# Layer 1 attention: four scheduled lanes become one list of 72 slots, with the engines held to the order of the text

## The chip, the cores and the metric

The kernel runs on one core of one Trainium2 chip. A core has five engines with instruction queues of their own: TensorE (PE, with its weight loads shown apart as PEld), VectorE (DVE), ScalarE (ACT), GpSimd (POOL) and SyncE (SP, which issues most transfers). The metric is the device time in microseconds: the median of the runs of one kernel. A profile is one execution, taken by the hardware profiler.

## The reference, cut to what matters

The program is a trunk of two layers on 1024 frames of width 1024. The change lies in layer 1, chunked softmax attention of 16 heads of 64, each chunk of 64 frames against itself and the 8 chunks before it:

```
qkv = (h @ w_qkv).reshape(bsz, seq, 3, C_HEADS, C_HEAD_DIM)
q = rmsnorm(qkv[:, :, 0], q_g) * (C_HEAD_DIM ** -0.5)
k = rmsnorm(qkv[:, :, 1], k_g)
v = qkv[:, :, 2]
...
s = jnp.einsum('bqhd,bkhd->bhqk', q_c, k_b).astype(jnp.float32) + bias
s = jnp.where(valid, s, -jnp.inf)
prob = jax.nn.softmax(s, -1).astype(v.dtype)
return jnp.einsum('bhqk,bkhd->bqhd', prob, v_b)
...
mix = chunk_band_attention(h, ...) @ attn_w_out[o]
x = x + mix
hf = rmsnorm(x, norm_ffn_g[i])
x = x + jnp.square(jax.nn.relu(hf @ mlp_w1[i])) @ mlp_w2[i]
x = x + rmsnorm(p[i] @ ple_w_proj[i], ple_norm_g[i]) * jax.nn.sigmoid(x @ ple_w_gate[i])
```

Numbers are split into a high and a low part of a narrower type, so a dense product is three matmuls (high by high, high by low, low by high), scores and values two.

## The kernel before, in words

Layer 1's input part is `layer1_in`. It works in 16 steps: `s = 2*pr + hf` is a pair of heads `pr` (0 to 7) and a half `hf` of the frames, four tiles of 128 frames. A step has four blocks, one for each head `h` of the pair and each half `blk` of the step, so there are 64 blocks, numbered `4*s + 2*h + blk`. A block takes two tiles of 128 queries (`m0` and `m0 + 1`), each against up to five tiles of 128 keys.

The work of a step, with the names that the trace shows:

- `attn_in`: the in-projection, four groups of 24 matmuls of 384 columns (`dps<-wq,act`). Each group is evicted by ACT (`qk`, line 1982, and `vs`, line 1986) and DVE (`vs`, line 1987). POOL squares q and k (`sq`, line 1994), DVE sums them (line 1995), makes one over the root with small instructions (lines 281 to 286) and multiplies (line 1998).
- `attn_norm`: eight PE transposes (`dps<-ident,qk`), first k, then q. For each, ACT makes the high part `F` (lines 2020 and 2022) and DVE the low part (line 2023: `F` for k, `Ql` for q).
- `attn_block`: for each of the two query tiles, the score matmuls into `sc`, then on DVE one custom instruction (line 2079) that adds the bias `toep` and takes the row minimum of the negated sum into `mx` (with a small read of the accumulator behind it), then the exponential on ACT (line 2081). Then PE transposes the probabilities in groups of up to 512 columns (`pt<-ident,pb`), ACT copies the high part and DVE the low part (`ptile`, lines 339 and 340), and PE multiplies them by the values into `po`. After the second block of a head `otmp` (ACT, line 2122) and `y` (DVE, line 2123) put the halves together; after the last block of a step four transposes of one over the row sums (`dps<-ident,rl`) and a multiplication (line 2132) finish `y`, which goes to memory.

The scores have one tile in the accumulation memory, two banks (`sc`); `po` has one bank, `pt` three, and two banks (`dps`) serve the in-projection, the q and k transposes, and the row-sum transposes.

What sets the order: `run` takes pieces from four generators (two lanes of blocks, one of norms, one of in-projections) by a clock of estimated latencies (the table `LAT`); what it writes down is then placed on each engine by the framework's scheduler, which goes by its own simulated times. Only the MLP, in `tail`, holds the engines to the order of the text, through the helper class `Pinned` and the flag `self.pinned`.

When the 64 groups of the in-projection are written, `attn_ins` goes on with the projection of the per-layer embedding (`ple_proj`, matmuls `dps<-act,wq` of 512 columns) and the out-projection (`out_early`), which needs the finished `y`; the MLP and the gate follow in `tail`. Ahead of it all `row_stats` makes the row norms of x from eight one-column matmuls (`dps<-ones,acc`), which read sums that POOL adds up at the end of layer 0 (line 1753).

## Time and profile before

| what | value |
|---|---|
| median of 3 runs | 3059.35 us (3057.58 to 3066.11) |
| the profiled execution's own time | 3059.3 us |
| its span, first to last instruction | 3057.6 us |
| PE busy over the span | 2948.1 us (96%) |
| first in-projection matmul of layer 1 | 1674.86 us |
| last values matmul starts its row of 11 | 2246.26 us |
| mean granted TensorE clock | 0.977 |

Times of the trace count from the first instruction. A matmul's row gives its own duration, but matmuls overlap: a row of n equal ones has one start every (row time less one duration) / (n - 1). "Idle before" is time in which an engine did nothing, with the instruction whose end let it go on; a wait shorter than the last matmul's own duration does not show as idle.

### The profile page before, as it was taken

Reading aid. Unit: us, or ns where it says so; the run is one execution under the profiler, and the core shown is the slowest. Engines: PE = TensorE matmul, PEld = TensorE weight load, DVE = VectorE, ACT = ScalarE, POOL = GpSimd, SP = SyncE. Lnnn points to the kernel's source line nnn. Section 1 sums busy time; section 2 is a strip of 40 time slices with the busy share of each in tenths; the row PEclk is TensorE's granted clock in tenths of the full one; section 3 lists DMA queues with packets and bytes.
Section 4 is the critical chain, followed back from the end, with each engine's and each line's share of the span. In section 5 each row is a group of like instructions: output and inputs, shape, how many; then the busy total and the mean of one; then the engine's idle time right before and its main releaser. Section 6 shows DMA issues by size and latency. Waiting matters only on the chain. (4 is left out here: it accounts for less than half of the span.)

```text
span 3057.6 us, 44955 instructions
## 1 busy us (share of the span) xinstructions
PE 2948.1 (96%) x16792; PEld 2473.0 (81%) x16792; DVE 2153.9 (70%) x3440; ACT 1409.1 (46%) x2546; POOL 1266.6 (41%) x1412
## 2 busy tenths in 40 slices
PE   8999999999989999999999999999999999999999
PEld 6888778887877888788888889988887888788887
DVE  5766766567758888877676566666758888877672
ACT  4444443444435544543333466655645444543331
POOL 5545533445504666644445100000204666645442
PEclk9999989999999999999999999999999999999999
DMA  4222212222444434655323111110284443654322
GB/s 129 95 86 67 68 48 74 76 66 75 163 162 165 159 150 150 245 199 172 124 90 128 65 45 41 54 44 20 81 298 167 159 151 149 240 202 174 124 94 100
DMA packets 166763, 374.29 MB, mean 122 GB/s; under 512 B 41360, under 2 KB 45584, under 8 KB 165136
## 3 DMA queue, kind: packets, MB, share of 16 engines
q1 hardware_dynamic: 134288, 312.68, 29.7%
q10 hardware_dynamic: 32256, 58.73, 5.1%
q8 instruction: 132, 2.16, 0.3%
q14 instruction: 87, 0.71, 0.1%
HBM read 259.15 MB, written 112.20 MB: 121 GB/s over the span
## 5 line engine op out<-in xcount | busy, mean ns | idle before, releaser
L173 PE MATMUL dps<-r,act 128*128 128x512 f32 x4440 | 1045.2, 394 | 10.7 <-DVE act L113 8.6
L173 PEld LDWEIGHTS dps<-r,act 128*128 128x128 f32 x4440 | 835.5, 189 | 203.5 <-DVE act L113 17.4
L173 PE MATMUL dps<-xg,whi 128*128 128x512 f32 x1248 | 420.4, 415 | 16.4 <-ACT xg L342 8.1
L113 ACT CAST act<-late 128x512 fp32r<-128x512 f32 (+1 forms) x282 | 205.5, 731 | 447.2 <-DVE late L113 258.2
L113 DVE TENSOR_TENSOR act<-late,act 128x512 fp32r<-128x512 f32 (+1 forms) x282 | 332.7, 1181 | 72.5 <-ACT act L113 69.2
L173 PE MATMUL dps<-wq,act 128*128 128x384 f32 x1536 | 301.9, 344 | 7.7 <-DVE y L2132 3.4
L173 PEld LDWEIGHTS dps<-xg,whi 128*128 128x128 f32 x1248 | 236.9, 195 | 66.8 <-ACT xg L342 8.1
L173 PEld LDWEIGHTS dps<-wq,act 128*128 128x128 f32 x1536 | 265.1, 190 | 12.7 <-DVE vs L1987 4.6
L173 PE MATMUL dps<-xg,wlo 128*128 128x512 f32 x624 | 256.4, 411 | 0.0
L113 POOL TENSOR_TENSOR late<-late 128x512 f32<-128x512 f32 (+1 forms) x104 | 186.5, 1802 | 82.4 <-ACT late L113 59.8
L113 POOL TENSOR_TENSOR late<-late,rs 128x512 f32<-128x512 f32 x88 | 137.1, 1570 | 100.9 <-DVE late L113 92.9
L1994 POOL TENSOR_TENSOR sq<-qk 128x512 f32<-128x512 f32 x32 | 34.2, 1069 | 297.1 <-ACT qk L1982 287.8
L113 DVE TENSOR_TENSOR late<-late 128x512 f32<-128x512 f32 x120 | 142.2, 1185 | 1.0
L113 DVE TENSOR_TENSOR r<-act,r 128x1024 fp32r<-128x1024 f32 (+1 forms) x80 | 138.1, 1728 | 6.7 <-ACT r L113 6.7
L173 PE MATMUL dps<-xw,act 128*128 128x512 f32 x576 | 139.2, 394 | 3.4 <-ACT act L113 3.4
L173 PEld LDWEIGHTS dps<-xg,wlo 128*128 128x128 f32 x624 | 121.3, 194 | 25.2 <-issue 0.2
L2079 DVE CUSTOM_DVE_ANT_0 pb<-sc,toep 128x640 f32<-128x640 f32 (+4 forms) x128 | 83.7, 654 | 73.4 <-PE sc L173 72.8
L173 PEld LDWEIGHTS dps<-xw,act 128*128 128x128 f32 x576 | 108.8, 189 | 28.1 <-ACT act L113 3.8
L298 ACT CAST whi<-wraw 128x1024 fp32r<-128x1024 f32 x76 | 79.5, 1048 | 86.8 <-PE dps L173 49.4
L299 DVE TENSOR_TENSOR wlo<-wraw,whi 128x1024 fp32r<-128x1024 f32 x76 | 95.1, 1252 | 33.9 <-ACT whi L298 32.8
L113 DVE TENSOR_TENSOR late<-late,dps 128x512 f32<-128x512 f32 x154 | 104.7, 682 | 19.3 <-ACT late L113 16.6
L2081 ACT ACTIVATE pb<-pb,mx 128x640 f32<-128x640 f32 (+4 forms) x128 | 89.5, 700 | 61.7 <-DVE mx L2079 55.2
(504 smaller groups left out, 5748.3 us busy)
## 6 DMA issues: line engine op xcount, KB each, us to landing
late<-in_w SPq DMA_DIRECT2D x100, 512.0 KB
hc<-late ACTq DMA_DIRECT2D x154, 256.0 KB
act<-hc SPq DMA_DIRECT2D x76, 512.0 KB
wraw<-in_w_in SPq DMA_DIRECT2D x56, 512.0 KB
hraw<-hc SPq DMA_DIRECT2D x36, 512.0 KB
hc<-sums ACTq DMA_DIRECT2D x70, 256.0 KB
act<-in_w SPq DMA_DIRECT2D x28, 512.0 KB
wraw<-in_w_out SPq DMA_DIRECT2D x21, 512.0 KB
```

The costliest lines, as they stand in the source:

```text
L113: return lambda *args, **kw: self.tc.keep_in_program_order(f(*args, **kw))
L173: r = self.nc.tensor.matmul(out, lhsT, rhs, start=start, stop=stop)
L298: nc.scalar.copy(hi, raw)
L299: nc.vector.tensor_tensor(lo, raw, hi.bitcast(F32), op=ALU.subtract)
L1994: G.tensor_tensor(sq, q4[:, 8 * e:8 * e + 8], q4[:, 8 * e:8 * e + 8], op=ALU.mult)
L2079: V.tensor_tensor_reduce(S, ps[:, o:o + n * P], toep[:, (5 - n) * P:], op0=ALU.add, op1=ALU.min, scale=-1.0, scalar=-NEG, accum_out=mx)
L2081: A.activation(S, S, AF.Exp, bias=mx, scale=-1.0, accum_out=st["l"][:, m % 4, h:h + 1])
```

## The change

The four generators go. A new function, `attention`, writes the stage as one list of 72 full slots, k from -8 to 63, and a short last one. Slot k holds the values of block k-1, the transposes of block k, the scores of block k+1, and one group of the in-projection (number k+8), whose eight pieces of three matmuls are put between the others by `fill`. When the 64 groups are used up, `fill` takes pieces of the embedding projection and then of the out-projection. Evictions, weight splits, bias loads, q and k norms and the finishing of `y` have fixed slots. Every compute instruction of PE, DVE, ACT and POOL in `attention` that goes through `self.mm`, `self.tr` or the pinned handles keeps the order of the text; the late weight and embedding work is not pinned on DVE, ACT and POOL. Three things move between engines or tiles: the small norm instructions and the scaling of q and k go from DVE to POOL (`norms`), in two halves, k first; the transposes of q, k and the row sums go from the `dps` banks to the three `pt` banks; and the eviction of v's high part is ahead of that of q and k.

```diff
     def tr(self, out, in_, ident):
         self.now += 0.107
-        return self.nc.tensor.transpose(out, in_, ident)
+        r = self.nc.tensor.transpose(out, in_, ident)
+        return self.tc.keep_in_program_order(r) if self.pinned else r
...
-            jobs = iter([(s, h, b) for s in range(16) for h in range(2) for b in range(2)])
-            self.run([self.attn_lane(steps, jobs, l1) for _ in range(2)] + [self.attn_norms(steps, l1), self.attn_ins(steps, l1)])
-
-    def attn_ins(self, steps, l1):
...
+            self.attention(l1)
...
+    def attention(self, l1):
...
+        def w_split(pr, j):
+            if j == 0:
+                W[pr] = self.weights3(pr % 2)
+            hi, lo = (w[:, j, :] for w in W[pr])
+            raw = raws.pop((pr, j))
+            A.copy(hi, raw)
+            V.tensor_tensor(lo, raw, hi.bitcast(F32), op=ALU.subtract)
...
+        def dense(d):
+            hf, e = d // 4 % 2, d % 4
+            wh, wl = W[d // 8]
+            ps = dps[d] = self.bank([P, 3, P])
+            ts = slice((4 * hf + e) * P, (4 * hf + e) * P + P)
             for k in range(NK):
...
+        def evict(d):
+            s, e = d // 4, d % 4
...
             A.activation(hi, v3, AF.Copy, scale=rc)
+            A.activation(st["qk"][:, e, :], ps[:, 0:2, :].rearrange("p a c -> p (a c)"), AF.Copy, scale=rc)
             V.scalar_tensor_tensor(vf[:, 1:3, :], v3, rc, hi.bitcast(F32), op0=ALU.mult, op1=ALU.subtract)
...
+        def squares(s, e):
+            q4 = ST[s]["qk"].rearrange("p i c -> p (i c)").rearrange("p (n d) -> p n d", d=64)
+            sq = ST[s]["sq"] = wp.tile([P, 8, 64], F32, tag="sq", name="sq", bufs=1)
             G.tensor_tensor(sq, q4[:, 8 * e:8 * e + 8], q4[:, 8 * e:8 * e + 8], op=ALU.mult)
...
+        def sums(s, e):
+            V.tensor_reduce(ST[s]["ss"][:, 8 * e:8 * e + 8], ST[s]["sq"], op=ALU.add, axis=AX.X)
+
+        def norms(s):
+            st = ST[s]
+            ss = st["ss"]
+            nn = sm.tile([P, 16], F32, tag="nn1", name="nn1")
+            w = sm.tile([P, 16], F32, tag="rswq", name="rsw")
+            G.tensor_scalar(ss, ss, 1.0 / 64, 1e-6, op0=ALU.mult, op1=ALU.add)
+            G.tensor_scalar(nn.bitcast(I32), ss.bitcast(I32), -0.5, 1597463007.0, op0=ALU.mult, op1=ALU.add)
+            for _ in range(3):
+                G.tensor_tensor(w, nn, nn, op=ALU.mult)
+                G.tensor_tensor(w, w, ss, op=ALU.mult)
+                G.tensor_scalar(w, w, -0.5, 1.5, op0=ALU.mult, op1=ALU.add)
+                G.tensor_tensor(nn, nn, w, op=ALU.mult)
+            q5 = st["qk"].rearrange("p i (j h d) -> p i j h d", j=2, h=2)
+            n4 = nn.rearrange("p (i j h) -> p i j h", i=4, j=2)
+            for j in (1, 0):
+                n = n4[:, :, j, :].rearrange("p i (h o) -> p i h o", o=1).broadcast_to((P, 4, 2, 64))
+                G.tensor_tensor(q5[:, :, j], q5[:, :, j], n, op=ALU.mult)
+
+        def bank():
+            return psm.tile([P, HB], F32, tag="pt", name="pt", bufs=3)
+
+        def heads(s, j):
+            st, qk = ST[s], ST[s]["qk"]
+            g = self.vec("kg") if j else self.dv["qg8"]
+            pt = bank()
...
+            for h in range(2):
+                r, o = halves[h], halves[1 - h]
+                A.activation(F[r, h], pt[r], AF.Copy, scale=g[r])
+                V.scalar_tensor_tensor(F[o, h] if j else lo[h][r], pt[r], g[r], F[r, h].bitcast(F32),
+                                       op0=ALU.mult, op1=ALU.subtract)
+            if not j:
+                for h in range(2):
+                    r, o = halves[h], halves[1 - h]
+                    A.activation(F[o, h], pt[r], AF.Copy, scale=g[r])
...
+        def scores(k, w):
...
+            pb = wp.tile([P, 5 * P], F32, tag="pb", name="pb", bufs=4)
+            V.tensor_tensor_reduce(pb[:, 0:n * P], ps[:, off * P:(off + n) * P], toeps[s // 2, h][:, (5 - n) * P:],
+                                   op0=ALU.add, op1=ALU.min, scale=-1.0, scalar=-NEG, accum_out=mx)
+            jb["probs"][w] = (pb, f0, mx, n, m)
+
+        def exps(k, w):
...
+            A.activation(pb[:, 0:n * P], pb[:, 0:n * P], AF.Exp, bias=mx, scale=-1.0,
+                         accum_out=ST[jb["s"]]["l"][:, m % 4, h:h + 1])
+
+        def turn(k, b):
...
+            A.copy(t[:, 0, u], pt[:, u])
+            jb["pts"][b] = (t, pt, u)
+
+        def low(k, b):
+            jb = JOB[k]
+            if b < len(jb["used"]):
+                t, pt, u = jb["pts"][b]
+                V.tensor_tensor(t[:, 1, u], pt[:, u], t[:, 0, u].bitcast(F32), op=ALU.subtract)
...
+        def values(k):
...
+        def outs(k):
...
+            A.copy(tmp[r], po[o])
+            V.tensor_tensor(st["y"][r], po[r], tmp[r], op=ALU.add)
+
+        def weigh(s):
...
+            V.reciprocal(st["l"], st["l"])
+            G.tensor_copy(rl.rearrange("p m (h i) -> p (m h) i", h=2), st["l"].rearrange("p m (h o) -> p (m h) o", o=1)
+                          .broadcast_to((P, 8, 64)))
...
+        def finish(s):
+            st = ST[s]
+            pn = bank()
+            for m in range(4):
+                self.tr(pn[:, m * P:(m + 1) * P], st["rl"][:, m, :], self.ident)
+            V.tensor_tensor(st["y"], st["y"], pn, op=ALU.mult)
...
+        def filler():
+            for d in range(64):
+                yield from dense(d)
+            yield from ple()
+            yield from out_first()
+        fl = [filler(), None]
+
+        def fill(n=1):
+            while n:
+                if fl[1] is not None and fl[1] not in self.done:
+                    return False
+                r = next(fl[0], "end")
+                if r == "end":
+                    return False
+                fl[1] = r if isinstance(r, tuple) else None
+                n -= fl[1] is None
+            return True
+
+        has = lambda k: 0 <= k < 64
...
+        for k in range(-8, 65):
+            pr, c = (k + 16) // 8, (k + 16) % 8
+            fill()
+            if has(k + 7):
+                evict(k + 7)
+            if pr < 8 and c in (1, 3, 5):
+                w_load(pr, c // 2)
+            if pr < 8 and c in (3, 5, 7):
+                w_split(pr, c // 2 - 1)
+            for h, q in ((0, k + 7), (1, k + 3)):
+                if q % 8 == 0 and has(q):
+                    toep_load(q // 8, h)
+            for h, q in ((0, k + 5), (1, k + 1)):
+                if q % 8 == 0 and has(q):
+                    toep_mask(q // 8, h)
...
+            if k % 4 == 3 and k > 0:
+                weigh(k // 4)
+            fill()
+            if has(k - 1):
+                values(k - 1)
+            fill()
+            if has(k - 1) and k % 2 == 0:
+                outs(k - 1)
+                if k % 4 == 0:
+                    finish(k // 4 - 1)
+            if k % 4 == 2 and has(k + 2):
+                heads((k + 2) // 4, 0)
+            if has(k + 5) and k % 4 == 3:
+                squares((k + 5) // 4, 0)
+            if has(k + 4) and k % 4 == 0:
+                squares((k + 4) // 4, 1)
+            if has(k + 1):
+                scores(k + 1, 0)
+            fill()
+            if has(k):
+                turn(k, 0)
+            if has(k + 1):
+                exps(k + 1, 0)
+            fill()
+            if has(k):
+                low(k, 0)
+            if has(k + 1):
+                scores(k + 1, 1)
+            if has(k + 5) and k % 4 == 3:
+                sums((k + 5) // 4, 0)
+            if has(k + 4) and k % 4 == 0:
+                sums((k + 4) // 4, 1)
+                norms((k + 4) // 4)
+            fill()
+            if has(k):
+                turn(k, 1)
+            fill()
+            if has(k):
+                turn(k, 2)
+            if has(k + 1):
+                exps(k + 1, 1)
+            if has(k):
+                low(k, 1)
+                low(k, 2)
+            if k % 4 == 1 and has(k + 3):
+                heads((k + 3) // 4, 1)
+            fill()
+            if k == -8:
+                ps = bank()
+                for i in range(NT):
+                    self.mm(ps[:, i:i + 1], self.accs[i // 4][:, (i % 4) * P:(i % 4 + 1) * P], self.ones[:, 0:1],
+                            start=True, stop=True)
+                self.row_norms(ps, self.rscol)
+        while ("ylast", 0) not in self.done:
+            fill()
+        self.split_scaled(self.ylast, ST[15]["y"], None, slice(0, HB))
+        self.done["at", 15] = 0
+        while fill():
+            pass```

The order that this gives, at the places that the prediction speaks of. In it `sc` are scores, `pt<-ident,pb` transposes of probabilities, `po` values, `dps<-wq` the in-projection, and ISA a custom instruction (with its small read behind it).

DVE, around the low parts of q (`Ql`) of one step, before:

```order
L2023 SCALAR_TENSOR_TENSOR F_17406<-dps,vecs,F_17406 64x512
L340 TENSOR_TENSOR ptile<-pt,ptile 128x512
L340 TENSOR_TENSOR ptile<-pt,ptile 128x384
L2023 SCALAR_TENSOR_TENSOR Ql<-dps,d_qg_85,F_17419 64x512
L2123 TENSOR_TENSOR y<-po,otmp 64x512
L2079 ISA pb,mx<-sc,toep 128x640
L2079 ISA mx 128x1
L2132 TENSOR_TENSOR y<-y,dps 128x512
L2023 SCALAR_TENSOR_TENSOR Ql<-dps,d_qg_85,F_17419 64x512
L2079 ISA pb,mx<-sc,toep 128x640
```

and now, in slot k with k % 4 == 2 and the slot behind it:

```order
L113 SCALAR_TENSOR_TENSOR F_18815<-pt,vecs,F_18815 64x512 x2
L113 SCALAR_TENSOR_TENSOR vs<-dps,rscol,vs 128x128
L113 TENSOR_TENSOR y<-po,otmp 64x512
L113 SCALAR_TENSOR_TENSOR Ql<-pt,d_qg_85,F_18853 64x512 x2
L113 ISA pb,mx<-sc,toep 128x384
L113 ISA mx 128x1
L113 TENSOR_TENSOR ptile<-pt,ptile 128x384
L113 ISA pb,mx<-sc,toep 128x512
L113 ISA mx 128x1
L113 SCALAR_TENSOR_TENSOR vs<-dps,rscol,vs 128x128
L113 TENSOR_TENSOR wq_18906<-wraw,wq_18905 128x1024
L113 RECIPROCAL l<-l 128x8
```

Before, a score's custom instruction stands between the two halves of q's low part; now both halves stand ahead of it, and the split of a weight stands ahead of the first custom instruction of the slot behind.

PE, around the transposes of k and then q (`dps<-ident,qk`), before:

```order
L178 MATMUL dps<-ident,qk 128x128 x4
L173 MATMUL sc<-F_18437,F_18835 128x512
L173 MATMUL sc<-F_18437,Ql 128x512
L173 MATMUL sc<-F_18822,F_18835 128x128
L173 MATMUL sc<-F_18822,Ql 128x128
L178 MATMUL pt<-ident,pb 128x128 x7
L178 MATMUL dps<-ident,qk 128x128 x4
L173 MATMUL po<-ptile,vs 128x256
L173 MATMUL sc<-F_18437,F_18835 128x384
```

and now, around those of q:

```order
L178 MATMUL pt<-ident,qk 128x128 x4
L173 MATMUL sc<-F_19176,F_19218 128x384
L173 MATMUL sc<-F_19176,Ql 128x384
L173 MATMUL dps<-wq_18905,act 128x384
L173 MATMUL dps<-wq_18906,act 128x384
L173 MATMUL dps<-wq_18905,act 128x384
L178 MATMUL pt<-ident,pb 128x128 x3
L173 MATMUL dps<-wq_18905,act 128x384
L173 MATMUL dps<-wq_18906,act 128x384
L173 MATMUL dps<-wq_18905,act 128x384
L173 MATMUL sc<-F_19176,F_19218 128x512
```

Before, the pieces of a block stood next to each other where the scheduler had spent the in-projection elsewhere; now six in-projection matmuls and a group of transposes stand between the two halves of the scores, in every slot.

PE, in slots 60 and 61, now (what stands ahead of them is the embedding projection):

```order
L173 MATMUL dps<-ones,act 128x1 x8
L173 MATMUL po<-ptile,vs 128x256 x6
L173 MATMUL po<-ptile,vs 128x128 x2
L178 MATMUL pt<-ident,rl 128x128 x4
L173 MATMUL sc<-F_20616,F_21072 128x256
L173 MATMUL sc<-F_20616,Ql 128x256
L173 MATMUL sc<-F_21015,F_21072 128x384
L173 MATMUL sc<-F_21015,Ql 128x384
L178 MATMUL pt<-ident,pb 128x128 x4
L173 MATMUL sc<-F_20616,F_21072 128x128
```

Nothing of another kind stands between the scores and transposes of these two slots; before, matmuls of the embedding projection (`dps<-act,wq`) did.

431 lines of the change are left out of this document (229 added, 202 removed).

## The prediction

> **What bounds the kernel now.** I read the page first, then stage windows around the changed function, then the waits of PE, then single timelines.
>
> ```profile
> PE 2948.1 (96%) x16792; PEld 2473.0 (81%) x16792; DVE 2153.9 (70%) x3440; ACT 1409.1 (46%) x2546; POOL 1266.6 (41%) x1412
> ```
>
> ```profile
> 1674.00:1691.00 17.00, 12.52 (x61) 11.63 (x60) 10.76 (x20) 6.14 (x10) 9.07 (x14) 0.80 0.63 214
> 1691.00:2176.00 485.00, 458.51 (x2950) 436.68 (x2950) 323.05 (x773) 282.46 (x628) 44.69 (x71) 1.00 0.12 40
> 2176.00:2249.00 73.00, 65.49 (x345) 54.87 (x344) 55.89 (x110) 43.46 (x83) 21.40 (x17) 0.93 0.53 193
> 2129.00:2132.90 3.90, 2.45 (x16) 1.81 (x15) 3.18 (x6) 3.25 (x6) 0.00 (x0) 1.00 0.00 0
> 2132.90:2136.30 3.40, 3.40 (x11) 3.40 (x12) 1.35 (x3) 0.92 (x2) 0.00 (x0) 0.50 0.20 77
> ```
>
> The columns are the length, busy PE, PEld, DVE, ACT, POOL, granted clock, transfers. PE bounds the whole program. In the changed stage it sits idle for 4.5 + 26.5 + 7.5 = 38.5 us. DVE (67%) and ACT (58%) are far from full in the long middle window. The last two rows show that a thin stretch (2.45 us busy of 3.9) is followed by one at half clock.
>
> More is lost than the idle time shows, since a short wait hides under the previous matmul. So I compare the stage with what its matmuls take in streams. These are the counts, and the timeline rows that give the rates:
>
> ```profile
> L173 PE MATMUL dps<-wq,act x1536: 331/336/689, 1674.9 to 2174.9; 128*128 128x384 f32 x192
> L173 PE MATMUL dps<-act,wq x336: 387/393/775, 2176.4 to 2291.6; 128*128 128x512 f32 x168
> ```
>
> ```profile
> L178 PE MATMUL pt<-ident,pb 128*128 128x128 f32 x480 | 82.9, 278 | 5.8 <-ACT pb L2081 5.8
> L178 PE MATMUL dps<-ident,qk 128*128 128x128 f32 x128 | 19.9, 275 | 2.2 <-ACT sq L1792 1.3 <-DVE vs L1987 0.9
> L178 PE MATMUL dps<-ident,rl 128*128 128x128 f32 x64 | 9.9, 274 | 1.2 <-DVE F L2023 1.2
> ```
>
> ```profile
> 1674.86 4.67 PE L173 MATMUL dps<-wq,act 128*128 128x384 f32 x24 [0.65 <-ACT gw L1737]
> 1680.21 1.05 PE L173 MATMUL dps<-ones,acc 128*128 128x1 f32 x8 [0.68 <-POOL acc L1753]
> 1684.15 1.86 PE L173 MATMUL dps<-ones,acc 128*128 128x1 f32 x8 [2.88 <-POOL acc L1753]
> 1686.27 5.76 PE L173 MATMUL dps<-wq,act 128*128 128x384 f32 x24 [0.26 <-DVE ms L374]
> 1693.24 21.07 PE L173 MATMUL dps<-wq,act 128*128 128x384 f32 x120 [1.21 <-DVE vs L1987]
> ...
> 2012.28 0.28 PE L173 MATMUL sc<-F,F 128*128 128x256 f32 x1
> ...
> 2012.87 0.51 PE L173 MATMUL dps<-wq,act 128*128 128x384 f32 x2
> ...
> 2164.34 0.64 PE L173 MATMUL po<-ptile,vs 128*128 128x256 f32 x4
> ...
> 2168.33 0.60 PE L178 MATMUL dps<-ident,rl 128*128 128x128 f32 x4
> ...
> 2247.48 44.53 PE L173 MATMUL dps<-act,wq 128*128 128x512 f32 x192
> ```
>
> Rates: an in-projection matmul (21.07 - 0.34)/119 = 0.174 us; a transpose (0.60 - 0.27)/3 = 0.11; a full score of 1,280 columns (high and low part) 2012.87 - 2012.28 = 0.59; 256 columns of values (0.64 - 0.28)/3 = 0.12; a matmul of 512 columns (44.53 - 0.39)/191 = 0.231. Scores and values have 122,880 columns each by the code (7,680 for each of 16 heads). The sum to 2247.48: 1,536 x 0.174 = 267; 672 x 0.11 = 74; scores 96 x 0.59 = 57; values 480 x 0.12 = 58; 144 of the 336 wide ones x 0.231 = 33; one-column sums 3. That is 492 us of 2247.48 - 1674.86 = 572.6. So **81 us** is the most that any order can win here, and the profiled time without it is 2978.
>
> **The change part by part.** PE's matmuls stay the same in number and shape, and so does nearly all work of ACT. DVE loses the small norm instructions and the scaling; in the middle window DVE has 162 us to spare, so this alone is worth nothing. What counts is what is left of the 81 us. A slot with five key tiles for each query tile has 24 x 0.174 + 2 x 0.59 + values of 1.2 + 10 x 0.11 = 7.6 us of PE work, and a third or so less in the shorter blocks. Other engines must keep that pace, and each hand-off must fit its distance in the text.
>
> **The short distance is between the two halves of the scores.** They share one tile, so the second half waits for the first half's custom instruction on DVE. Between them PE has 3 + 3 in-projection matmuls (1.04 us) and at most four transposes (0.44): 1.48 us.
>
> ```profile
> L2079 DVE CUSTOM_DVE_ANT_0 pb<-sc,toep 128x640 f32<-128x640 f32 x64 | 52.5, 820 | 38.5 <-PE sc L173 38.1
> L2079 DVE DVE_READ_ACCUMULATOR2_ANT mx<- 128x1 f32 x128 | 10.6, 83 | 0.0
> L1945 ACT CAST wq<-wraw 128x1024 fp32r<-128x1024 f32 x19 | 19.3, 1050 | 4.9 <-DMA wraw<-in_w_qkv 4.8
> L1946 DVE TENSOR_TENSOR wq<-wraw,wq 128x1024 fp32r<-128x1024 f32 x19 | 23.2, 1221 | 4.0 <-ACT wq L1945 3.6
> L1982 ACT ACTIVATE qk<-dps,rscol 128x256 f32<-128x256 f32 x64 | 30.4, 474 | 71.1 <-PE dps L173 68.3 <-PE sc L173 2.1
> ```
>
> The custom instruction takes 0.82 + 0.08, with hand-offs about 1.0, so DVE has some 0.45 us of room, if it is free when the scores end. Three kinds of slot put something ahead.
>
> Slots with k % 4 == 2 (15 with scores) have q's transposes straight ahead of the scores, and DVE's order has both low parts of q ahead of the custom instruction. Those form a chain with ACT, which a quiet place (k, the same shapes) shows:
>
> ```profile
> 1714.97 0.67 ACT L2020 ACTIVATE F<-dps,vecs 64x512 fp32r<-64x512 f32 x1
> 1715.67 0.75 DVE L2023 SCALAR_TENSOR_TENSOR F<-dps,vecs,F 64x512 fp32r<-64x512 f32 x1 [0.21 <-ACT F L2020]
> 1716.45 0.68 ACT L2020 ACTIVATE F<-dps,vecs 64x512 fp32r<-64x512 f32 x1 [0.81 <-DVE F L2023]
> 1717.17 0.76 DVE L2023 SCALAR_TENSOR_TENSOR F<-dps,vecs,F 64x512 fp32r<-64x512 f32 x1 [0.75 <-ACT F L2020]
> ```
>
> ACT's second high part waits for DVE's first low part, so the chain is serial: 1717.93 - 1714.97 = 2.96 us. With the custom instruction 3.96; PE covers 0.59 + 1.48 = 2.07. **Stall 1.9 us, 15 times: 29 us.** Behind the waiting scores stand the slot's remaining in-projection pieces, and ACT's copies of q for the other head stand ahead of its exponentials; both fit before the next slot's values. Bounds: nothing, if ACT and DVE catch up (I see no slack for that), and 2.6 us each (39), if ACT comes late from k's transposes one slot earlier.
>
> Slots with k % 8 == 3 (six) have a weight split ahead of the first custom instruction. ACT arrives about 1.3 us late from the slot before (my estimate from its stall), then evicts (0.65), casts (1.05), DVE subtracts (1.22), then 1.0: 5.2 us. PE, with short values there, asks at 1.04 + 0.35 + 0.52 + 0.59 + 1.48 = 3.98. Stall 1.3 each: **8 us**, between 0 and 12. In the splits at 5 and 7 the values are longer (1.2 in place of 0.35), which hides it.
>
> **The start** stays: the sums wait for POOL (0.68 + 2.88 us above) and the next 24 matmuls take 5.76 in place of 4.2, together **5 us**; the waits on the eviction behind them go, since a group now has a whole slot for it.
>
> **The tail.** Slots 60 and 61 have nothing to fill with: the embedding projection is used up and the out-projection waits for `y` of step 14. The eight one-column sums stand on PE ahead of block 59's values and wait for the last addition on POOL:
>
> ```profile
> L1794 POOL TENSOR_TENSOR act<-act,sq 128x512 f32<-128x512 f32 x14 | 18.3, 1307 | 31.0 <-ACT sq L1792 31.0
> ```
>
> I put 2.5 us for that, 2 for each of the two bare slots, and 1.7 for a stretch at half clock like the one above: **8 us**, between 4 and 15. [...]
>
> **POOL** now makes the norms: 14 small instructions, then a multiplication for k. Their cost depends on DVE:
>
> ```profile
> 971.77 0.69 DVE L113 TENSOR_TENSOR act<-act 128x512 f32<-128x512 f32 x1
> 971.88 0.64 POOL L276 TENSOR_TENSOR rsw<-col 128x8 f32<-128x8 f32 x1
> 977.00 0.20 POOL L276 TENSOR_TENSOR rsw<-col 128x8 f32<-128x8 f32 x1
> 977.28 0.20 POOL L277 TENSOR_TENSOR rsw<-rsw,ms 128x8 f32<-128x8 f32 x1
> L1994 POOL TENSOR_TENSOR sq<-qk 128x512 f32<-128x512 f32 x32 | 34.2, 1069 | 297.1 <-ACT qk L1982 287.8 <-PE pt L178 9.3
> ```
>
> With an idle DVE one takes 0.28 start to start; beside DVE additions from the main memory on chip it takes 0.64. In the attention, POOL's `sq` keeps 1.07 beside DVE's work, so I take 0.28: 14 x 0.28 + 1.1 = 5.0 us, against 5.2 from the sums' end to k's transposes in the tightest slot. It just fits: **0**.
>
> **Short waits** that I cannot place: the old order had about 81 - 38.5 = 42 us not seen as idle, some 7 of it half clock. A regular order should have fewer; I take **10**, bounds 0 and 36.
>
> Sum left: 29 + 8 + 5 + 8 + 10 = 60, a gain of 81 - 60 = 21. Against the profiled execution (3059.3, a span of 3057.6 and 1.7 around it): **3038 us**. The median shown is 3059.35, so nothing has to be moved.
>
> **The rivals.**
>
> *A clean rotation (0.15).* If the chain behind q's transposes is taken up by ACT and DVE running ahead, 23 us remain (start 5, tail 8, short waits 10): 3059.3 - 58 = 3001. For it: DVE and ACT are under 70% busy. Against: in a fixed order neither can start before the transposes.
>
> *Waits that only change place (0.20).* If the short waits persist (36 in place of 10): 3038 + 26 = 3064, in effect no change. For it: PE still visits the same tiles in small groups.
>
> *Slower: the custom instruction is late in every slot (0.17).* The place is the same, the room 0.45 us. Besides the 21 slots above, some 43 have a y addition, a y multiplication or a split ahead of it. If DVE reaches the first score 1.5 us after it is done, each loses 1 us: 3038 + 43 = 3081. It decides from 0.45 us on. For it: 1,221 ns of a split or 686 ns of an addition exceed the room. Against: by my working those fall before the scores end.
>
> *POOL late with k's norms (0.08).* At 0.6 us an instruction the chain is 14 x 0.6 + 1.3 = 9.7 us, k's transposes wait 4.5 in the short slot and 1.6 in the long one, 8 times each: 3038 + 49 = 3087. It needs DVE to hold POOL up throughout. [...]
>
> **How the numbers follow.** Forecast 0.40, rivals 0.15, 0.20, 0.17, 0.08. The forecast's own range is 3025 to 3050. About 0.3% (9 us) is what a measurement can tell from no change: faster 0.40 + 0.15 = 0.55, same 0.20, slower 0.25. The range takes in the clean rotation and the two slow cases as far as their prices: 3002 to 3088.
>
> **What would show it.** Right: PE waits on DVE's custom instruction in the slots with q's transposes, about 1.9 us, 15 times, and hardly elsewhere; transposes of k wait for POOL nowhere; stage length from 572.6 to some 552 us; half clock at the start and near slots 60 to 62. Wrong: such waits in most slots, POOL's small norm instructions over 0.4 us, or PE waiting on ACT copies (`ptile`) or on `po`.

## The result and the profile after

The changed kernel is **slower: 3078.81 us median of 5 runs (3072.76 to 3086.85) against 3059.74 us of 5 runs (3057.58 to 3066.11), a ratio of 1.006 with a 95% interval of 1.0039 to 1.0082.** The forecast was 3038 us, faster. The profiled execution took 3075.75 us, with a span of 3074.0.

I cut the changed stage at the same pieces of work in both kernels: the first in-projection matmul, the first of the ninth group, the first of the 57th, the last one, and the start of the last values matmul. So the four parts are a start, a middle of six times eight groups, a last eight groups, and a tail. The stretches of the kernel before (length, then busy PE, PEld, DVE, ACT, POOL, granted clock, transfers):

```profile
1674.90:1721.20 46.30, 39.72 (x217) 38.17 (x217) 20.64 (x45) 13.35 (x27) 12.84 (x18) 0.93 0.27 91
1721.20:2110.60 389.40, 369.06 (x2401) 351.12 (x2401) 269.22 (x643) 236.45 (x524) 35.87 (x61) 1.00 0.13 43
2110.60:2174.90 64.30, 60.90 (x385) 57.91 (x384) 42.27 (x102) 36.89 (x84) 5.06 (x8) 0.97 0.07 25
2174.90:2247.40 72.50, 64.99 (x347) 54.60 (x345) 56.29 (x110) 43.27 (x84) 21.40 (x17) 0.93 0.52 190
```

The same stretches of the changed kernel:

```profile
1672.60:1722.30 49.70, 42.46 (x221) 40.61 (x222) 20.06 (x38) 15.96 (x32) 15.98 (x29) 0.88 0.25 84
1722.30:2111.10 388.80, 360.26 (x2361) 343.81 (x2361) 233.99 (x483) 233.97 (x507) 101.44 (x254) 0.99 0.13 43
2111.10:2179.40 68.30, 63.02 (x398) 60.08 (x397) 39.54 (x84) 39.32 (x88) 15.88 (x42) 0.95 0.13 44
2179.40:2267.10 87.70, 71.31 (x368) 58.70 (x367) 58.29 (x106) 48.04 (x93) 28.69 (x33) 0.92 0.51 184
```

The stage takes 594.5 us in place of 572.5, that is 22 more. The rest of the program gives back some 6: the stage starts 2.3 us earlier here, and what follows it, which begins with the rest of the out-projection, is 3.3 us shorter. The middle is as long as before, the start and the last eight groups are 3.4 and 4.0 us longer, and **the tail is 15.2 us longer**.

Where PE waits in the middle (total us, times, longest): the two largest of ten kinds in the kernel before, and the only kind in the changed one:

```profile
PE po L173 <- ACT ptile L339: 5.3, 8, 1.1
PE pt L178 <- ACT pb L2081: 4.9, 12, 1.1
```

```profile
PE sc L173 <- DVE mx L113: 28.5, 18, 2.2
```

The many short waits of the kernel before, on probabilities, evictions and low parts, are gone. What is left as idle time is one wait, of the second score half for the first half's custom instruction. In a slot with q's transposes the timeline of PE shows it, and that of DVE the reason:

```profile
2062.62 0.60 PE L178 MATMUL pt<-ident,qk 128*128 128x128 f32 x4
2062.98 0.42 PE L173 MATMUL sc<-F,F 128*128 128x384 f32 x1
...
2064.17 0.77 PE L173 MATMUL dps<-wq,act 128*128 128x384 f32 x3
2066.95 0.50 PE L173 MATMUL sc<-F,F 128*128 128x512 f32 x1 [2.01 <-DVE mx L113]
...
2074.00 0.44 PE L173 MATMUL sc<-F,F 128*128 128x384 f32 x1 [0.56 <-DVE mx L113]
```

```profile
2064.05 0.74 DVE L113 SCALAR_TENSOR_TENSOR Ql<-pt,d_qg,F 64x512 fp32r<-64x512 f32 x1
2065.55 0.76 DVE L113 SCALAR_TENSOR_TENSOR Ql<-pt,d_qg,F 64x512 fp32r<-64x512 f32 x1 [0.75 <-ACT F L113]
2066.33 0.56 DVE L113 CUSTOM_DVE_ANT_0 pb<-sc,toep 128x384 f32<-128x384 f32 x1
2066.82 0.08 DVE L113 DVE_READ_ACCUMULATOR2_ANT mx<- 128x1 f32 x1
```

The scores begin at 2062.98 and take some 0.6 us, and the custom instruction starts at 2066.33, behind both low parts of q. The pattern repeats in every pair of steps: 2.01 us, 0.56 in the next slot (a weight split ahead of the custom instruction), 2.19 four slots later.

In the tail, the waits are of many kinds:

```profile
PE sc L173 <- DVE mx L113: 6.9, 4, 3.5
PE dps L173 <- POOL act L2198: 4.2, 1, 4.2
PE dps L173 <- ACT sq L2196: 2.2, 3, 1.3
PE pt L178 <- POOL qk L113: 1.4, 1, 1.4
PE dps L173 <- ACT act L2196: 1.2, 2, 0.8
```

The longest is the one-column sums, which stand on PE until POOL's additions are made; the two bare slots follow. PE, then POOL:

```profile
2229.30 3.84 PE L173 MATMUL dps<-ones,act 128*128 128x1 f32 x16 [4.23 <-POOL act L2198]
...
2239.65 0.48 PE L173 MATMUL sc<-F,F 128*128 128x128 f32 x1 [2.59 <-DVE mx L113]
```

```profile
2226.97 2.27 POOL L2198 TENSOR_TENSOR act<-act,sq 128x512 f32<-128x512 f32 x1 [2.23 <-ACT sq L2196]
2229.95 1.26 POOL L2198 TENSOR_TENSOR act<-act,sq 128x512 f32<-128x512 f32 x1 [0.71 <-ACT sq L2196]
```

**What a narrow matmul costs.** The prediction counted 0.12 us for 256 columns and half of that for 128. A values block of the changed kernel at a place without waits shows otherwise, and so does a narrow pair of scores:

```profile
2047.45 1.50 PE L173 MATMUL po<-ptile,vs 128*128 128x256 f32 x12
2048.80 0.74 PE L173 MATMUL dps<-wq,act 128*128 128x384 f32 x3
2049.38 0.60 PE L178 MATMUL pt<-ident,rl 128*128 128x128 f32 x4
...
2055.79 0.22 PE L173 MATMUL sc<-F,F 128*128 128x128 f32 x1
...
2055.96 0.74 PE L173 MATMUL dps<-wq,act 128*128 128x384 f32 x3
2056.53 0.60 PE L178 MATMUL pt<-ident,pb 128*128 128x128 f32 x4
```

The row of twelve is eight values matmuls of 256 columns and four of 128 (the view joins them). By columns it should take 1.20 us and the three in-projection matmuls behind it 0.52; they take 1.35 and 0.58, so each narrow one costs 0.05 us more than its columns. The pair of scores takes 0.17 in place of 0.12, with the same 0.05 on the group behind. So a matmul of 128 columns takes some 0.11 us, as a transpose does. There are 288 of them (192 values, 96 scores), which adds some 13 us: the streams of the stage take 505 us, not 492, and the kernel before loses **67.5 us, not 81**. What sets the spacing of 0.11 us was not tested by a run.

With this rate for narrow matmuls and the prediction's for the others, I take each part's length less what its own matmuls need. This is the loss of each part in us, the experiments beside the two kernels. The parts are those of the profiled execution, which is not always near the median of all runs in the last column (e1_qlow 3051.8 us, e6_free 3034.4).

| kernel | start | middle | last eight | tail | sum | median us |
|---|---|---|---|---|---|---|
| before | 10.3 | 35.0 | 7.4 | 14.8 | 67.5 | 3059.7 |
| changed | 13.2 | 39.4 | 9.9 | 26.8 | 89.3 | 3078.8 |
| e1_qlow | 13.1 | 15.0 | 3.8 | 23.5 | 55.4 | 3041.4 |
| e2_tail | 12.4 | 37.1 | 9.9 | 23.2 | 82.6 | 3070.0 |
| e7_sums | 12.6 | 37.4 | 10.0 | 23.7 | 83.7 | 3072.9 |
| e4_norms_dve | 10.6 | 52.8 | 9.9 | 27.8 | 101.1 | 3091.2 |
| e3_all | 12.6 | 7.7 | 5.3 | 19.2 | 44.8 | 3030.5 |
| e8_pe_held | 9.2 | 10.5 | 1.7 | 20.1 | 41.5 | 3032.2 |
| e10_pe_held_all | 9.1 | 10.3 | 1.7 | 13.3 | 34.4 | 3026.4 |
| e6_free | 9.5 | 22.1 | 3.1 | 8.2 | 42.9 | 3026.5 |
| e11_tail_free | 12.7 | 8.6 | 3.6 | 5.4 | 30.3 | 3017.7 |

### The profile page after: what moved, and what is told of

Same layout as the page of the kernel before. It is cut to its first block, busy times and chain, and to the rows that moved or that the text cites. A ratio compares the mean times of both kernels' runs of the same rounds, so it can differ in the third digit from the quotient of the medians.

```text
span 3074.0 us, 45073 instructions
## 1 busy us (share of the span) xinstructions
PE 2947.6 (96%) x16792; PEld 2472.8 (80%) x16792; DVE 2112.4 (69%) x3248; ACT 1412.6 (46%) x2546; POOL 1355.1 (44%) x1668
## 5 line engine op out<-in xcount | busy, mean ns | idle before, releaser
L173 PE MATMUL dps<-r,act 128*128 128x512 f32 x4440 | 1045.2, 394 | 13.1 <-DVE act L113 8.5
L173 PEld LDWEIGHTS dps<-r,act 128*128 128x128 f32 x4440 | 836.5, 189 | 204.6 <-DVE act L113 15.2
L173 PE MATMUL dps<-xg,whi 128*128 128x512 f32 x1248 | 419.7, 414 | 14.1 <-ACT xg L343 6.9
L113 ACT CAST act<-late 128x512 fp32r<-128x512 f32 (+1 forms) x282 | 205.5, 731 | 442.9 <-DVE late L113 258.1
L113 DVE TENSOR_TENSOR act<-late,act 128x512 fp32r<-128x512 f32 (+1 forms) x282 | 330.0, 1172 | 71.5 <-ACT act L113 68.2
L173 PE MATMUL dps<-wq,act 128*128 128x384 f32 x1536 | 340.9, 353 | 1.1 <-ACT gw L1738 0.9
L173 PEld LDWEIGHTS dps<-xg,whi 128*128 128x128 f32 x1248 | 236.3, 195 | 64.8 <-ACT xg L343 6.8
L173 PEld LDWEIGHTS dps<-wq,act 128*128 128x128 f32 x1536 | 264.4, 193 | 4.8 <-ACT gw L1738 1.3
L173 PE MATMUL dps<-xg,wlo 128*128 128x512 f32 x624 | 256.3, 411 | 0.0
L113 POOL TENSOR_TENSOR late<-late 128x512 f32<-128x512 f32 (+1 forms) x104 | 187.8, 1813 | 81.4 <-ACT late L113 58.4
L113 POOL TENSOR_TENSOR late<-late,rs 128x512 f32<-128x512 f32 x88 | 137.5, 1575 | 101.5 <-DVE late L113 94.0
L113 DVE TENSOR_TENSOR r<-act,r 128x1024 fp32r<-128x1024 f32 (+1 forms) x80 | 139.2, 1741 | 6.7 <-ACT r L113 6.7
L113 DVE TENSOR_TENSOR late<-late 128x512 f32<-128x512 f32 x120 | 142.3, 1186 | 1.0
L173 PEld LDWEIGHTS dps<-xg,wlo 128*128 128x128 f32 x624 | 121.2, 194 | 25.7 <-DVE wlo L300 0.4
L173 PE MATMUL dps<-xw,act 128*128 128x512 f32 x576 | 137.8, 392 | 0.0
L113 ACT CAST ptile<-pt 128x512 fp32r<-128x512 f32 (+1 forms) x144 | 74.0, 515 | 134.7 <-PE pt L178 134.3
L113 DVE TENSOR_TENSOR ptile<-pt,ptile 128x512 fp32r<-128x512 f32 (+1 forms) x144 | 83.9, 600 | 68.2 <-ACT ptile L113 67.2
L173 PEld LDWEIGHTS dps<-xw,act 128*128 128x128 f32 x576 | 108.4, 188 | 24.2
L113 DVE TENSOR_TENSOR late<-late,dps 128x512 f32<-128x512 f32 x154 | 104.6, 682 | 19.7 <-ACT late L113 15.9
L113 ACT ACTIVATE late<-late 128x512 f32<-128x512 f32 x176 | 110.6, 631 | 13.5 <-POOL late L113 9.8
```

The lines of the kernel that those rows point to most:

```text
L113: return lambda *args, **kw: self.tc.keep_in_program_order(f(*args, **kw))
L173: r = self.nc.tensor.matmul(out, lhsT, rhs, start=start, stop=stop)
```

## The experiments

Ratios are against the kernel before on the same chip, with 95% intervals. Medians of different runs are compared across chips, on which the kernel before took 3058.0 to 3062.1 us, so a difference of some 4 us between two medians means little by itself.

### q's low parts behind the custom instruction (e1_qlow)

```diff
+        def q_low(s):
+            ...
+                V.scalar_tensor_tensor(st["Ql"][h][r], st["qpt"][r], g[r], st["Q"][r, h].bitcast(F32),
+                                       op0=ALU.mult, op1=ALU.subtract)
...
             if has(k + 1):
                 scores(k + 1, 0)
+            if k % 4 == 2 and has(k + 2):
+                q_low((k + 2) // 4)
             fill()
...
                 exps(k + 1, 0)
+            if k % 4 == 2 and has(k + 2):
+                q_other((k + 2) // 4)
```

> Edit: ACT's two high parts of q stay ahead of the scores, DVE's two low parts of q move behind the first custom instruction of the slot, and ACT's two copies for the other head go behind the first exponential. Theory (the changed kernel's steady loss is the custom instruction standing behind q's low parts, 2.01 and 2.19 us, 15 times): these 15 waits go, eight slots take 64.75 - 4.2 - 0.2 = about 60.4 us, the time falls by 30 to 36 us, to 3043 to 3049. Rival (the old and the changed kernel both take 64.8 us for eight slots, so something common to both bounds them): PE then waits elsewhere, on the low parts of the probabilities or on the exponentials, eight slots stay at 64 to 65 us and the time at 3074 to 3081.

Measured: 3041.39 us, ratio 0.9955 (0.9933 to 0.9976). Eight slots take 60.9 us. The waits of PE in the middle, and DVE in a slot with q's transposes:

```profile
PE sc L173 <- DVE mx L113: 7.2, 6, 1.2
```

```profile
1993.25 0.54 DVE L113 CUSTOM_DVE_ANT_0 pb<-sc,toep 128x384 f32<-128x384 f32 x1
1993.72 0.07 DVE L113 DVE_READ_ACCUMULATOR2_ANT mx<- 128x1 f32 x1
1994.05 1.51 DVE L113 SCALAR_TENSOR_TENSOR Ql<-pt,d_qg,F 64x512 fp32r<-64x512 f32 x2 [0.25 <-ACT F L113]
```

The two long waits of each pair of steps are gone, and nothing took their place. The wait in the slot with the first weight split grew from 0.56 to 1.2 us, since PE now comes to it earlier. **The theory holds and the rival of a common bound falls**: that the old and the changed kernel both take 64.8 us for eight slots is chance. This edit alone is worth 34 us by the stage's loss and 37 by the medians; the time is 1.6 us below the expected range.

### The projection spread and the sums later (e2_tail), the sums alone (e7_sums)

```diff
+            spread, place = (), [0]
+            if 56 <= k <= 59:
+                spread = (2, 7, 8)
+            if 60 <= k <= 61:
+                spread = (2, 8)
+
+            def fill():
+                place[0] += 1
+                if place[0] not in spread:
+                    fill_all()
...
                 yield from self.dense_part(w, y, ev, self.order)
+                if n == 0:
+                    self.row_stats([self.pacc[:, 0, :], self.pacc[:, 1, :]], self.prsc)
```

The last two lines are the edit of e7_sums; e2_tail has both.

> Edit: the 32 pieces of the embedding projection are spread over slots 56 to 61 (5, 5, 5, 5, 6, 6) in place of 8 in each of slots 56 to 59, and its eight one-column sums stand behind the first output tile of the out-projection. Theory (the tail loses some 27 us because projection pieces come faster than ACT, POOL and DVE clear them, then the sums hold PE 4.2 us for POOL, then two slots are bare): from the last in-projection matmul to the last values the 88.0 us become 68 to 72, and the time falls by 16 to 20 us, to 3059 to 3063. Rival (the tail waits come from DVE's and ACT's own load, the weight and y splits of these slots): 82 us or more, 3073 to 3081.

> Edit: of the tail's two edits in e2_tail only one: the eight one-column sums stand behind the first output tile of the out-projection; the pieces are not spread. Theory (the sums hold PE 4.2 us for POOL ahead of block 59's values, and bring a stretch at half clock): 4 to 6 us faster than the changed kernel, 3073 to 3075, and the spreading alone is worth the other 3 to 5 of e2_tail's gain. Rival (the two bare slots behind the sums wait for DVE and ACT all the same): within 2 us of the changed kernel.

Measured: e2_tail 3069.95 us, ratio 1.0030 (1.0017 to 1.0042); e7_sums 3072.92 us, ratio 1.0033 (1.0023 to 1.0042). By the medians the sums are worth 6 us, as expected, but their tail loses only 3.1 us less; 2.0 of the rest lies in the middle, which the edit does not touch. The spreading is worth 3 by the medians and 1.1 by the stage's loss, and the two intervals overlap, so that it is worth anything is not shown; 10 or more had been left for it. The tail of e2_tail takes 84.2 us in place of 87.7, where the theory said 68 to 72 and the rival 82 or more; the time fell into neither range. Its waits:

```profile
PE pt L178 <- POOL qk L113: 5.4, 1, 5.4
PE sc L173 <- DVE mx L113: 5.0, 2, 2.5
```

The wait for the sums (4.2) went, and k's transposes of step 15 now wait 5.4 us for POOL in place of 1.4. The tail is a chain of short distances; here the cure at one place showed the next.

### Both, and the first weight split behind the scores (e3_all)

```diff
             if pr < 8 and c in (5, 7):
                 w_split(pr, c // 2 - 1)
...
             if has(k + 1):
                 scores(k + 1, 1)
+            if pr < 8 and c == 3:
+                w_split(pr, 0)
```

> Edit: both edits above, and the first of each three weight splits stands behind the slot's second score half. By the two theories the gains add: 30 to 36 + 16 to 20 + 7 x 0.6 = 50 to 60 us, 3019 to 3029. If the cure of one only uncovers the other's wait, less than 40, 3040 or more. By the two rivals 3070 to 3080.

Measured: 3030.49 us, ratio 0.9913 (0.9891 to 0.9935). It is 48 us faster than the changed kernel, where 50 to 60 were expected; what is missing is the tail's share. Eight slots take 59.9 us. One such stretch, with PE, PEld, DVE, ACT and POOL as above:

```profile
1896.40:1956.30 59.90, 59.78 (x398) 57.35 (x397) 39.00 (x82) 39.13 (x85) 16.75 (x42) 1.00 0.13 47
```

PE is busy for 59.78 of 59.90 us, and the loss by my count is some 1.3 us. **The rotation that the change wanted does exist in this text; in its steady part it was three pieces of DVE's work away from it**, with the ACT copies of q that moved along.

### The norms back on DVE (e4_norms_dve)

```diff
-            G.tensor_scalar(ss, ss, 1.0 / 64, 1e-6, op0=ALU.mult, op1=ALU.add)
+            V.tensor_scalar(ss, ss, 1.0 / 64, 1e-6, op0=ALU.mult, op1=ALU.add)
...
-                G.tensor_tensor(w, nn, nn, op=ALU.mult)
+                V.tensor_tensor(w, nn, nn, op=ALU.mult)
```

> Edit: the 14 small instructions of the norms go back from POOL to DVE, the two multiplications stay on POOL. Theory (POOL's norms fit, they cost only 1.2 us once at the start and 1.4 us once in the tail): within 4 us of the changed kernel, 3075 to 3083; DVE's 14 instructions of some 0.2 us may lengthen a wait for the custom instruction in the slots that hold them. [...]

Measured: 3091.24 us, ratio 1.0103 (1.0086 to 1.0119), 12 us slower than the changed kernel. The theory (within 4) was wrong. PE's waits in the middle, and DVE in a slot with norms:

```profile
PE sc L173 <- DVE mx L113: 28.5, 18, 2.2
PE po L173 <- DVE ptile L113: 7.0, 6, 1.2
```

```profile
1897.37 0.17 DVE L113 TENSOR_SCALAR ss<-ss 128x16 f32<-128x16 f32 x1
...
1900.08 0.17 DVE L113 TENSOR_TENSOR nn<-nn,rsw 128x16 f32<-128x16 f32 x1
1900.18 1.01 DVE L113 TENSOR_TENSOR ptile<-pt,ptile 128x512 fp32r<-128x512 f32 x2
```

The 14 small instructions take 1900.18 - 1897.37 = 2.8 us in one piece, ahead of the low parts of the probabilities, and the values wait 1.2 us for these, six times. The wait for the custom instruction is what it was in the changed kernel; the 7.0 us are new, and the clock stands at half for 15.5 us of this middle in place of 5.3. DVE is busy 65% of the middle here. So the move of the small norm instructions to POOL, which the prediction priced at nothing, is worth 12 us in this order: it is not DVE's total that matters but what stands ahead of the instruction that PE waits for.

### The late splits at fixed places (e5_late), and the projection's evictions too (e5p_late)

```diff
+            if 58 <= k <= 60:
+                y_split(k - 58, 0)
+            if k in (57, 59):
+                late_split(k // 2 - 27)
+                late_load(k // 2 - 26)
```

These lines stand behind the second score half. In both, the casts and subtractions of these splits go through the helpers that keep the text's order; in e5p_late the evictions, squares and additions of the projection do too.

> Edit: on top of all the edits of e3_all, the splits of the late weights and of y stand at fixed places in the text (behind the second score half of slots 57 to 60) and keep it, in place of wherever DVE and ACT took them up. Theory (what the tail still loses, 19 us there, comes from bursts of these splits on DVE and ACT ahead of custom instructions and of the sums for the norms of step 15): the tail becomes 70 to 75 us in place of 80.1, the time 3020 to 3026. Rival (DVE and ACT are simply loaded in these slots, so the waits change place): 78 us or more, 3028 to 3034.

> Edit: as e5_late, and the embedding projection's evictions, squares and additions keep the text's order too. Theory (they follow PE's order anyway): within 3 us of e5_late. Rival (held to the text they stop DVE or ACT behind a projection bank that is not ready): 4 us or more slower than e5_late.

Measured: e5_late 3036.86 us, ratio 0.9918 (0.9894 to 0.9941); e5p_late 3043.28 us, ratio 0.9939 (0.9918 to 0.9961). The tail of e5_late is 79.7 us against 80.1 of e3_all, inside the rival's range: in this tail the waits for the custom instruction fall from 3.2 us to 1.3, and the k transposes wait 5.6 us for POOL in place of 2.5. So placing the splits only moves the waits. (The median of e5_late is 6 us above e3_all's, but its stage is not longer; its four times spread over 14 us, and in the profiled one the stage began 14 us later. That difference is not explained.) With the projection held too, the tail grows to 89.1, and the time is 6.4 us above e5_late's, as that rival said. **Holding the projection's evictions too made the tail worse.**

### No engine held to the text (e6_free), PE alone held (e8_pe_held)

```diff
-        V, A, G = (Pinned(tc, e) for e in (nc.vector, nc.scalar, nc.gpsimd))
-        self.pinned, self.done = True, {}
+        V, A, G = nc.vector, nc.scalar, nc.gpsimd
+        self.pinned, self.done = False, {}
```

In e8_pe_held the flag stays True, so that PE keeps the text's order.

> Edit: the changed kernel, its text as it is, but no engine is held to the text's order; the scheduler places each instruction. Theory (the loss is the order of the text on DVE, q's low parts ahead of the custom instruction; a scheduler that is free puts what is ready first): the waits for the custom instruction become fewer, eight slots take 62 to 64 us, 3050 to 3070. Rival (the scheduler follows the text anyway): 64.7 us and 3075 to 3081. Second rival (without the fixed order PE's pieces bunch up, as in the kernel before): waits of many kinds, 3060 to 3100.

> Edit: the changed kernel, its text as it is; PE keeps the text's order, DVE, ACT and POOL are placed by the scheduler. In the DVE order that comes of it the custom instruction stands ahead of both low parts of q. Theory (only DVE's and ACT's fixed order costs in the steady part; PE's order is harmless): the waits of 2.0 and 2.2 us go, eight slots take 60 to 62 us, the time is 3035 to 3050, and it stays above the version in which PE is free too (3026) by what the tail loses with PE held (the two bare slots and the sums). Rival (PE's fixed order is itself the cost, and the version with all engines free won by moving PE's pieces): 64 us and 3065 to 3080.

Measured: e6_free 3026.47 us, ratio 0.9879 (0.9862 to 0.9895), better than expected; e8_pe_held 3032.23 us, ratio 0.9918 (0.9893 to 0.9943), slightly better than expected. The same text without the fixed order is 52 us faster than with it. DVE in a slot with q's transposes, in e8_pe_held, and all that PE waits for in its middle:

```profile
2009.57 0.81 DVE L2049 CUSTOM_DVE_ANT_0 pb<-sc,toep 128x640 f32<-128x640 f32 x1
2010.31 0.08 DVE L2049 DVE_READ_ACCUMULATOR2_ANT mx<- 128x1 f32 x1
2010.31 0.74 DVE L2000 SCALAR_TENSOR_TENSOR Ql<-pt,d_qg,F 64x512 fp32r<-64x512 f32 x1
...
2012.55 0.76 DVE L2000 SCALAR_TENSOR_TENSOR Ql<-pt,d_qg,F 64x512 fp32r<-64x512 f32 x1
```

```profile
PE sc L173 <- DVE mx L2049: 5.4, 6, 1.0
```

The scheduler puts the custom instruction ahead of q's low parts by itself. The table tells PE's order from that of the other three together: with DVE, ACT and POOL free and PE held, the middle's loss falls from 39.4 to 10.5, the start's from 13.2 to 9.2, and the tail's only from 26.8 to 20.1. With PE free too, the tail loses 8.2, but the middle 22.1: PE's even turns are worth having in the middle (10.5) and harmful in the tail. Eight slots take 60.3 us with PE held, and some 62 with it free once they run evenly (the first three of the middle's six eights take 41.9, 68.3 and 65.0).

### The better text, all free (e9_free_all) or PE held (e10_pe_held_all)

The text is that of e3_all, with the lines just shown.

> Edit: the text of e3_all (q's low parts and the first weight split behind the custom instructions, the projection spread, the sums later), no engine held to it. Theory (the scheduler already makes these moves by itself): the same as the free version of the changed kernel, 3022 to 3031. Rival (the better text leads the scheduler to a better order): 3010 to 3020.

> Edit: the text of e3_all, only PE is held to it. Theory (PE's even turns have a floor that e3_all reaches already, 59.9 us for eight slots; DVE and ACT gain in the tail when they are free): 3020 to 3030, tail 70 to 80 us. Rival (free engines bunch the splits ahead of custom instructions): slower than e3_all's 3030.

Measured: e9_free_all 3032.96 us, ratio 0.9915 (0.9896 to 0.9933); e10_pe_held_all 3026.38 us, ratio 0.9894 (0.9876 to 0.9912). The free scheduler makes nothing better of the better text; the time is 2 us above the range of its theory, and 6.5 above e6_free's. With PE held, the better text leaves the middle as it was and takes 20.1 - 13.3 = 6.8 us off the tail's loss; there the clock is at half for 3.4 us in place of 13.7.

### The better text held, all free from slot 54 (e11_tail_free)

```diff
             pr, c = (k + 16) // 8, (k + 16) % 8
+            if k == 54:
+                V, A, G = nc.vector, nc.scalar, nc.gpsimd
+                self.pinned = False
             fill()
```

It has the edits of e1_qlow and the moved weight split, but neither of the tail's.

> Edit: q's low parts and the first weight split stand behind the custom instructions as in e3_all; the projection is not spread and the sums stand where the changed kernel has them; from slot 54 on no engine is held to the text. Theory (what the tail loses is PE's fixed order there, so the scheduler fills the bare slots without a change of the text): the steady part stays at 59.9 us for eight slots, the tail loses some 8 us in place of 23, the time is 3015 to 3024 and this is the fastest of all. Rival (the tail's loss comes from the load of DVE, ACT and POOL in these slots, and the free kernel's small loss there from blocks that it left over on the way): the tail still loses 18 us or more, 3029 to 3036.

Measured: **3017.72 us, ratio 0.9863 (0.9837 to 0.9889), the lowest median of all**, 1.4% below the kernel before and 61 us below the changed one. Its interval overlaps those of e6_free and e10_pe_held_all, so that it is faster than these two is not shown by the times; its stage has the smallest loss in the table, 30.3 us. Middle, last eight groups and tail:

```profile
1721.90:2080.00 358.10, 357.27 (x2362) 342.64 (x2362) 231.76 (x483) 234.04 (x508) 101.78 (x254) 1.00 0.14 47
2080.00:2138.70 58.70, 56.18 (x368) 53.92 (x367) 37.28 (x77) 36.59 (x82) 15.88 (x42) 1.00 0.15 51
2138.70:2215.40 76.70, 73.49 (x428) 62.60 (x427) 59.44 (x115) 50.97 (x100) 27.22 (x34) 1.00 0.69 245
```

The tail has 428 matmuls where the changed kernel had 368: the blocks are left to run later, beside the projection and the out-projection, and there is no stretch at half clock. The loss there is 5.4 us, where the same text held throughout (e1_qlow, which lacks only the moved weight split) loses 23.5. So most of the tail's loss comes from the fixed order, and it goes together with blocks that run later; the two are not told apart. Which of its single waits would be the dearest, these runs don't tell, since with the order kept each cure showed another wait.

## Why the prediction was wrong, step by step

The sum was 60 us left of 81. By the table it is 89.3 left of 67.5. Two steps failed above all, the tail (15 us) and the budget (13), and then the start (8).

- **The budget** (81 us) is the first step that failed. The streams were counted by columns, and 288 narrow matmuls take 0.11 us, not 0.06. (The rate for the scores was read from a pair of 256 and 384 columns, which holds no narrow matmul.) That is 13 us, an estimate from this spacing, which no order can win, and the "short waits" of the old order had hidden them.
- **The short distance between the score halves** was right in place and nearly in size. q's chain: 1.9 us, 15 times, 29 in all; measured 2.01 or 2.2 us in most, 3.0 and 3.5 in two, 33.9 in 15. The weight split: 1.3 us, six times; measured 0.56, 3.3 in all. Together 37.2 where 37 stood. e1_qlow shows the cause, and that the whole of it was to be had.
- **The start** (5): measured 13.2. The wait for POOL's sums was as shown; the custom instruction of slot -1 (2.3 us), k's first transposes (1.2) and a stretch at half clock came on top. In the kernel before, the same part lost 10.3 already, so the step was too small in both.
- **The tail** (8, between 4 and 15): measured 26.8, of which 3.5 is q's chain of the last step. This is the largest miss. The sums cost 3.1 by the tail of e7_sums and 6 by its median, not 2.5. The clock is at half for 13.7 us of this tail, with PE busy for 13.5 of them, which is up to 6.8 us lost where 1.7 was priced. I had priced the bare slots, and not that ACT, POOL and DVE get the projection's evictions, the norms of step 15 and the splits of y in the same four slots, beside the attention's own instructions, which are held to the text (the projection's and the splits are not).
- **POOL** (0): right in the steady part. An instruction took 0.30 us start to start, and k's transposes wait for POOL only twice, 1.2 us in the start and 1.4 in the tail. But "this alone is worth nothing" of DVE's relief was wrong by 12 us (e4_norms_dve).
- **Short waits** (10): 15.6 in the middle and the last eight groups, of which three stretches at half clock make some 5.
- Put together: 13 (budget), 15 (tail without q's chain), 8 (start), 6 (short waits and half clock) make 42 of the 43 us from 21 us faster to 22 us slower in the stage.

Of the rivals, none was it. The time is close to that of *the custom instruction late in every slot* (3081), but the trace has that wait in the 21 places that were forecast and in four others, at the two ends of the stage, and not in every slot. *Waits that only change place* names the middle by its sum (35.0 before, 39.4 after), by chance: 32 of the 39 fell with two small edits. *POOL late* did not happen in the steady part. The first sign that I had named, waits of about 1.9 us on the custom instruction in 15 slots, came true while the stage grew from 572.5 to 594.5 us, not down to 552: it told of one term only.

One question was not put: what the kernel before did with the same pieces. Its scheduler was free to put the custom instruction first, and PE waited for it twice in the whole stage, 1.9 us. The change gave the text's order to DVE, ACT and POOL too, and this, not the rotation, is what made it slower: with these three free (e8_pe_held), or with q's low parts alone moved (e1_qlow), it is faster than the kernel before.

## What to carry to other kernels

When an order is fixed, fix it on the engine that bounds the stage, and look on each other engine at what stands ahead of the instruction that the bound engine waits for: 1.5 us of work at the wrong side of one instruction, 15 times, cost some 34 us here, on an engine that was busy for 60% of the middle. Hold the order where the work repeats and let it go where it runs out: held to slot 53 and free from there left the smallest loss in the stage. And count a budget with the cost of the narrowest matmuls, by the spacing in a quiet place, before calling the rest a loss.

## What had not been expected of the hardware

Half clock does not follow from the length of a wait alone. In the changed kernel's trace every change of the granted clock lies on one grid of 3.41 us. Here are slices of that grid around two waits with the same length, 2.19 us (up to 1840.44) and 2.20 us (up to 2036.22):

```profile
1836.84:1840.26 3.42, 1.41 (x10) 1.05 (x8) 2.61 (x4) 1.77 (x4) 0.00 (x0) 1.00 0.01 2
1840.26:1843.67 3.41, 3.23 (x12) 2.94 (x12) 1.55 (x5) 2.18 (x4) 0.00 (x0) 0.50 0.00 0
2031.43:2034.84 3.41, 2.59 (x19) 2.24 (x17) 2.37 (x5) 2.22 (x4) 0.00 (x0) 1.00 0.00 0
2034.84:2038.25 3.41, 2.03 (x13) 1.91 (x14) 2.19 (x5) 2.85 (x6) 0.00 (x0) 1.00 0.00 0
```

The first wait lies almost whole in one slice, leaves 1.41 us of busy PE in it, and is followed by a slice at 0.50. The second is shared by two slices, which keep 2.59 and 2.03 us, and no half clock follows. A wait of 2.2 us thus costs up to 1.7 us more, now and then (an estimate: half of the slice of 3.41 us at 0.50).

The share of work can be read from the same grid. Seven slices of the stage that ran at full clock hold 1.41 us of busy PE or less, and half clock follows each; the next fuller one holds 1.47 us, and full clock follows it and all others but one (2.23 us from 1676.42, with one-column matmuls in it). In the fourteen traces of this case, between 1660 and 2260 us, half clock follows all 43 slices below 1.47 us, 19 of 46 between 1.47 and 1.85, and 8 of 2,267 above; since matmuls' ends are modelled, these shares are rough.
